# Four of sixteen gate blocks move into a Strassen pass of the values' stage, and ScalarE copies the keys' second low parts

## The chip, the cores and the metric

The kernel runs on one core of one Trainium2 chip. The metric is the device time of one execution in microseconds (us); below one microsecond, nanoseconds (ns) are used. A core has a matrix engine (TensorE, in the profile PE, its weight loads PEld), a vector engine (VectorE, DVE), a scalar engine (ScalarE, ACT), GpSimd (POOL) and a sync engine (SP) whose queue issues most DMAs. TensorE multiplies a stationary 128x128 block by a moving block of up to 128x512 and adds the result up in a PSUM bank; VectorE and ScalarE read results from there. Each engine takes its own instructions in the order of its program and waits for the others by semaphores.

## The reference

One decoder layer on x of 1024 tokens by 1024 channels, all in float32. What matters here is its beginning:

```python
h = rms_norm(x, pre_mix_g)
proj = h @ w_in            # 1024 x 8192 columns
qa, ka, va, qb, kb, vb, gates = split(proj)
...
g_a, g_b = split(sigmoid(gates))     # 2 x 1024 columns
mix = (g_a * ya + g_b * yb) @ w_mix_out
```

`qa`, `ka`, `va` (512 columns each) feed four heads of differential attention ("A"), `qb`, `kb`, `vb` (1536 each) three groups of dilated window attention ("B"). Queries and keys are rotated by tables of cosines and sines. The 2048 gate columns are used only after both attentions. A convolution-gated MLP follows.

## The kernel before, in words

**Precision.** Every operand of a large product is split into a high part, rounded to the matrix engine's fast format, and a low part, the rest. `split` (line 148) makes them: ScalarE copies to the high part (line 149), VectorE subtracts for the low part (line 146). `mm3` (lines 153 to 157) then issues three matmuls: high by high, low by high, high by low.

**Projections of queries, keys and gates.** `proj_t` takes 128 columns of `w_in` as the stationary side (a unit of 128 x 1024, loaded by `load_unit` in two halves of 256 KB, each split into slots of 128x512, of which there are 6), and streams the tokens of x, in two halves of 512, over 8 blocks of the inner dimension: 2 x 8 x 3 = 48 matmuls of 128x512. The result stands with its columns on the partitions. For a gate, `put_gate` (line 248) multiplies each half by the tokens' inverse norms, `rstd_row`, on VectorE and stores it to `gt_d` by a DMA on ScalarE's queue; there are 16 gates of 128 columns. For queries and keys, `rotated` copies the partner rows on ScalarE (line 684) and uses the tables on VectorE (lines 685 to 687). The banks of these products are the three of the pool `acc`.

**Values' stage.** All 2048 columns of the values (A's 512 and B's 1536) are computed first, by Strassen's scheme with seven products instead of eight: x is cut into four blocks (two halves of the tokens by two halves of the inner dimension) and the weight likewise. The sums of x's blocks, t2, t3 and t4, and their high and low parts are made once. The weight's sums are made on VectorE while the stage runs. There are two passes of 1024 columns. `steps_v` lists the steps: a step is one of the products p1 to p7, a pass i, and one of four blocks k of the inner dimension. In each step of these two passes x is the stationary side, in four blocks of 128 tokens, and 512 columns of the weight stream: 4 x 3 = 12 matmuls. `fetch_v` fetches the weights' blocks 8 to 10 steps ahead into 14 buffers (three tags of two in `rt`, and four tiles of two halves in `tb`), `ready_v` sums and splits them 5 steps ahead, `step_v` issues the matmuls, and at a product's last step `take_v` moves the results from PSUM to `quarter`, which `put_v` stores to `v_d` on POOL's queue. Some products go on in the bank of another without clearing it (p6 in p1's, p7 and p4 behind it, p3 in p5's), so a take has to be done before the next one starts there. While this stage runs, the norms of x, the rotation tables and a few other things are made as well, and the tables are stored. During the first steps p5 and p6 of the second pass, half of x is fetched anew and split again, since p5's operand stood in its place.

**After it.** The tables are loaded into the place where t4 stood. One gate runs (`START_GATES`), then head 0's projection `proj_a(0)`. Then come the four heads of attention A; between the pieces of each head's attention, `interleave` puts the projection of the next head (p), gates (g), and loads and splits of values (v, w, x, V) as the strings of `A_FILLS` say. Before head 3's last fills, the first projection of B (P) follows. Attention B has projections as its fill, with three gates (`B_GATES`) in its last step. Then come the mixing branches, which use the gates.

**Keys of A.** For a head's two key halves, `put_k` (line 735) writes k0 and k1, each with the same 64 rows twice, by four copies on ScalarE (lines 738, 739), and l0 and l1, the low parts, also twice, by four subtractions on VectorE (line 742).

**Order.** The functions write the instructions down with priorities (`tc.high_priority` lifts some), and the framework's scheduler then fixes each engine's order by a simulated timeline. So TensorE's order may differ from the written one, and matmuls of a fill stand where those of an attention piece would have to wait.

Of the kernel before, what the change touches and what calls it, by code (L numbers as in the profile page):

```python
# [15 lines left out]
F32 = mybir.dt.float32  # L16
# [33 lines left out]
START_GATES, A_FILLS, B_GATES = 1, ("gpgg", "gpvgg", "wgpgg", "xgPVgg"), 3  # L50
# [12 lines left out]
def plan():  # L63
# [7 lines left out]
    order += [GT + i * P for i in range(2 * KC)]  # L71
# [16 lines left out]
def trunk(ctx: ExitStack, tc: tile.TileContext, a, out):  # L88
# [344 lines left out]

    def lambda_scale():
# [10 lines left out]
    with ExitStack() as st_y:  # L445
# [6 lines left out]
        def turns(pattern, *ps):  # L452

            ks = [iter(range(4)) for _ in ps]
            return [(ps[c], 1, next(ks[c])) for c in pattern]

        steps_v += [("p1", 1, k) for k in range(4)] + turns((0, 0, 1, 0, 1, 0, 1, 1), "p5", "p6")
        steps_v += turns((0, 0, 1, 1, 1, 1, 0, 0), "p3", "p7") + [("p4", 1, k) for k in range(4)]
# [14 lines left out]

        def fetch_v(n):
# [3 lines left out]
            got_v[n] = [load_raw(a["w_v"][j * 4 + k][:, (2 * i + c) * 512 : (2 * i + c + 1) * 512], next(tags), parts=1 if n else 2)  # L478
                        for c, j in which]

        def ready_v(n, w=512):
            p, _, k = steps_v[n]
            raw = got_v.pop(n)
            src = wz[k] if p in ("p5", "p6", "p3") else raw[0]
# [9 lines left out]
            for c in range(0, 512, w):  # L494
                marks["ACT"] = split(*(t[:, c : c + w] for t in ready[n]), src[:, c : c + w])

        def take_v(p, i, m, ps):
# [3 lines left out]
            def copy(to, r):  # L501
                if i:
# [4 lines left out]
            def add(to, r):  # L507
                if i:
# [27 lines left out]

        quarter = {(0, i): new_y(f"a{i}") for i in range(2)}
        banks = {}

        def step_v(n):  # L540
            p, i, k = steps_v[n]
            x = xs_of[p]
            if p in ("p1", "p2", "p5") and k == 0:
                left = p == "p1"
                banks[left] = ([psum() for _ in range(3)] + [psum(F32, ps_o, "o")] if left else
                               [psum(F32, q, t) for q, t in ((ps_s, "s"), (pt, "pt")) for _ in range(2)])
            use = banks[p in ("p1", "p6", "p7", "p4")]
            wh, wl = ready.pop(n)
            for m in range(4):
                tk = slice(m * P, (m + 1) * P)  # L550
                mm3(use[m], x[0][:, k, tk], x[1][:, k, tk], wh, wl, k == 0 and p in ("p1", "p2", "p5"), k == 3, p in ("p6", "p7", "p4", "p3"))
            if k < 3:
                return
            with tc.high_priority(offset=80):
                for m in range(4):
# [58 lines left out]
        places_y = {("p6", 1): (1, "a0", yv), ("p5", 1): (3, "b3", yw), ("p4", 1): (2, "b2", yw)}  # L614
        quarter.update({(q, 0): new_y(f"b{q}", yw) for q in range(1, 4)})
        for n in range(8, len(steps_v)):
# [29 lines left out]
            if k == 3 and i and p in ("p1", "p7", "p4", "p3"):  # L646
                put_v({"p1": 0, "p7": 3, "p4": 2, "p3": 1}[p], 1, p == "p1")
            if (p, i) == ("p5", 1):

                again.append(load_raw(a["xT"][k][:, 512:], next(tags)))  # L650
            if (p, i) == ("p6", 1):
# [72 lines left out]
    def proj_a(h, res):  # L724
# [10 lines left out]
        def put_k(half, sl, ps):  # L735
# [4 lines left out]
            for part, kk, ll in ((u, k0, l0), (v, k1, l1)):  # L740
# [1006 lines left out]
```

## Time and profile before

| | us |
|---|---|
| median of 3 runs | 1703.26 (1700.04 to 1705.16) |
| the profiled execution | 1702.22 |
| its span, first to last instruction | 1700.3 |
| TensorE busy | 1683.2 |
| VectorE busy | 1346.2 |
| ScalarE busy | 887.9 |
| end of the values' stage | 161.9 |
| first score of attention A | 202.70 |

The profile is a hardware trace of one execution. A line of a group names the line of code, the engine, the operation, the tiles (out<-in), the shapes and how often it ran; behind the bar stand its busy time, the mean ns of one, and the engine's idle time before it with what ended that. A line of a stretch gives its bounds, its length, the busy time and count of each engine (PE, PEld, DVE, ACT, POOL), the granted clock, the share of the DMA engines, and GB/s. A line of the timeline gives start, duration, engine, line, operation and tiles, and in brackets the idle time before. A line of a fetch gives the queue, the count, the size and the median us from issue to landing. Matmuls overlap, so their durations are longer than the distance from one start to the next.

### The profile page before, as it was taken

How to read it: one execution, taken by the hardware profiler on the slowest of the kernel's cores; microseconds unless marked ns; L12 is line 12 of the kernel's file. 1: busy time of each engine (PE TensorE's matmuls, PEld its weight loads, DVE VectorE, ACT ScalarE, POOL GpSimd, SP SyncE). 2: the span in 40 equal slices, each digit the busy share in tenths (PEclk: the TensorE clock that was granted, in tenths of full speed). 3: DMA queues.
4: the chain of work that ended last, by engine and by line, in shares of the span. 5: the costliest groups of instructions: out<-in, count | busy, mean ns of one | idle time of the engine just before them, and what ended most of it. 6: DMA issues, size and time to landing. Idle time of an engine off the chain costs nothing.

```text
span 1700.3 us, 23030 instructions
## 1 busy us (share of the span) xinstructions
PE 1683.2 (99%) x8076; PEld 1408.5 (83%) x8076; DVE 1346.2 (79%) x2557; ACT 887.9 (52%) x1631; POOL 109.1 (6%) x174
## 2 busy tenths in 40 slices
PE   9999999999999999999999999999999999999997
PEld 7888888888888888888888788888888888888886
DVE  8795687877777776677756865899999989799977
ACT  7633575655544776667553433454444444355453
POOL 0031000000000000000123400300000000000000
PEclk9999999999999999999999999999999999999999
DMA  8767311213112213243675532122222222296524
GB/s 270 229 224 267 99 55 62 88 56 118 50 63 81 69 57 108 81 130 101 219 266 184 196 112 75 38 101 91 99 75 81 86 90 92 76 351 213 201 76 161
DMA packets 104451, 216.41 MB, mean 127 GB/s; under 512 B 12992, under 2 KB 22144, under 8 KB 104336
## 3 DMA queue, kind: packets, MB, share of 16 engines
q1 hardware_dynamic: 89296, 171.28, 30.3%
q0 software_dynamic: 10288, 35.28, 6.2%
q10 hardware_dynamic: 4752, 8.39, 1.3%
q8 instruction: 63, 1.03, 0.3%
q14 instruction: 52, 0.43, 0.1%
HBM read 167.05 MB, written 47.86 MB: 126 GB/s over the span
## 4 chain that ended last, share of the span: by engine, by line
PE 86%; DMA 5%; DVE 5%; issue 2%; ACT 1%; POOL 1%; SPq 0%; DVEq 0%; POOLq 0%; ACTq 0%
PE acc L155 19%; PE acc L157 19%; PE acc L156 19%; PE acc L1583 3%; PE acc L1582 3%; PE acc L1581 3%; PE o L710 2%; PE pt L697 2%; PE acc L1262 2%; PE acc L1261 2%; PE acc L1260 2%; PE o L713 1%; DVE wlo L146 1%; DMA raw<-in_w_v 1%; PE s L766 1%
## 5 line engine op out<-in xcount | busy, mean ns | idle before, releaser
L155 PE MATMUL acc<-xh,whi 128*128 128x512 f32 x768 | 304.2, 396 | 0.0
L157 PE MATMUL acc<-xl,whi 128*128 128x512 f32 x768 | 303.8, 396 | 0.0
L156 PE MATMUL acc<-xh,wlo 128*128 128x512 f32 x768 | 303.1, 395 | 0.0
L149 ACT ACTIVATE whi<-raw 128x512 fp32r<-128x512 f32 (+1 forms) x252 | 155.7, 626 | 183.7 <-PE acc L157 101.2
L146 DVE TENSOR_TENSOR wlo<-raw,whi 128x512 fp32r<-128x512 f32 (+1 forms) x252 | 182.2, 730 | 39.2 <-ACT whi L149 35.0
L157 PEld LDWEIGHTS acc<-xl,whi 128*128 128x128 f32 x768 | 144.4, 188 | 27.8
L156 PEld LDWEIGHTS acc<-xh,wlo 128*128 128x128 f32 x768 | 144.5, 188 | 27.6
L155 PEld LDWEIGHTS acc<-xh,whi 128*128 128x128 f32 x768 | 144.4, 188 | 27.5 <-DVE t L685 0.2
L155 PE MATMUL acc<-mh,whi 128*128 128x512 f32 x400 | 155.8, 390 | 0.3 <-ACT mh L149 0.3
L156 PE MATMUL acc<-mh,wlo 128*128 128x512 f32 x400 | 155.6, 389 | 0.0
L157 PE MATMUL acc<-ml,whi 128*128 128x512 f32 x400 | 155.3, 389 | 0.0
L684 ACT ACTIVATE t<-acc 64x512 f32<-64x512 f32 (+1 forms) x160 | 94.7, 592 | 58.9 <-PE acc L157 57.0
L1458 DVE TENSOR_TENSOR u<-acc,u 128x512 f32<-128x512 f32 x133 | 91.8, 695 | 23.2 <-PE acc L157 23.1
L149 ACT ACTIVATE whi<-s 128x512 fp32r<-128x512 f32 x76 | 46.9, 627 | 102.9 <-PE acc L157 88.7
L685 DVE TENSOR_TENSOR t<-acc,cos 128x512 f32<-128x512 f32 x64 | 44.2, 691 | 58.9 <-ACT t L684 56.4
L155 PEld LDWEIGHTS acc<-mh,whi 128*128 128x128 f32 x400 | 75.1, 188 | 16.2 <-ACT mh L149 0.5
L157 PEld LDWEIGHTS acc<-ml,whi 128*128 128x128 f32 x400 | 75.1, 188 | 15.6
L156 PEld LDWEIGHTS acc<-mh,wlo 128*128 128x128 f32 x400 | 75.1, 188 | 15.4
L1582 PE MATMUL acc<-whi,wlo 128*128 128x512 f32 x220 | 77.6, 390 | 0.0
L1581 PE MATMUL acc<-whi 128*128 128x512 f32 x220 | 76.3, 389 | 0.0
L1583 PE MATMUL acc<-wlo,whi 128*128 128x512 f32 x220 | 73.2, 390 | 0.0
L768 DVE CUSTOM_DVE_ANT_0 s<-s,mask_a 128x512 f32<-128x512 f32 (+3 forms) x96 | 52.0, 554 | 23.2 <-PE s L766 14.6
(389 smaller groups left out, 3953.9 us busy)
## 6 DMA issues: line engine op xcount, KB each, us to landing
raw<-in_w_in SPq DMA_DIRECT2D x96, 256.0 KB, 2.9
raw<-in_w_up SPq DMA_DIRECT2D x88, 256.0 KB, 2.7
raw<-in_w_v SPq DMA_DIRECT2D x71, 256.0 KB, 4.5
raw<-c_d SPq DMA_DIRECT2D x48, 256.0 KB, 3.8
c_d<-c SPq DMA_DIRECT2D x22, 512.0 KB, 2.8
raw<-in_w_down SPq DMA_DIRECT2D x37, 256.0 KB, 4.2
v_d<-yv POOLq DMA_DIRECT2D x32, 256.0 KB, 5.1
gt_d<-gate ACTq DMA_DIRECT2D x32, 256.0 KB, 2.2
```

The costliest lines, as they stand in the source:

```text
L146: eng.tensor_tensor(lo, src, hi.bitcast(F32), op=ALU.subtract)
L149: copy = nc.scalar.activation(hi, src, AF.Copy)
L155: nc.tensor.matmul(o, sh, mh, start=first, stop=False, skip_group_check=on)
L156: nc.tensor.matmul(o, sl, mh, start=False, stop=False, skip_group_check=on)
L157: nc.tensor.matmul(o, sh, ml, start=False, stop=last, skip_group_check=on)
L684: nc.scalar.activation(t1[dst], ps[src], AF.Copy)
L685: nc.vector.tensor_tensor(t2, ps, cos[:, sl], op=ALU.mult)
L768: nc.vector.tensor_tensor_reduce(out=s_sb[:, c0:c1], in0=ps, in1=mask, scale=1.0, scalar=-3.0e38, op0=ALU.add, op1=ALU.max, accum_out=mx[: ...
L1458: nc.vector.tensor_tensor(to, made(p), x, op=ALU.add)
L1581: nc.tensor.matmul(banks[m], gh[:, tk], wh, start=f == 0, stop=False)
L1582: nc.tensor.matmul(banks[m], gl[:, tk], wh, start=False, stop=False)
L1583: nc.tensor.matmul(banks[m], gh[:, tk], wl, start=False, stop=f == NH - 1)
```

## The change

The first 512 gate columns (gates 0 to 3) are no longer projected by `proj_t`. They are appended to the values' weight array (2560 columns instead of 2048) and computed in a third pass of the values' stage, i = 2, which is half as wide: 256 columns per block. In it the sides are exchanged. The weight's part is stationary, in two blocks of 128 columns, and 512 tokens stream, so that the result has the gates' layout: 2 x 3 = 6 matmuls of 128x512 in a step, 28 steps. It uses two banks of `acc` and two of `s`. Its results are multiplied by `rstd_row` in the new `put_g` and stored to `gt_d` on POOL's queue. The renewed half of x is fetched in the third pass instead of the second. `START_GATES` is gone, and heads 0, 2 and 3 have two gates instead of three among their fills. In `put_k` each low part is subtracted once on VectorE and its second copy is made by ScalarE from the first.

```diff
-START_GATES, A_FILLS, B_GATES = 1, ("gpgg", "gpvgg", "wgpgg", "xgPVgg"), 3
+A_FILLS, B_GATES = ("gpg", "gpvgg", "wgpg", "xgPVg"), 3
...
-    order += [GT + i * P for i in range(2 * KC)]
+    order += [GT + i * P for i in range(4, 2 * KC)]
...
-        steps_v += [("p1", 1, k) for k in range(4)] + turns((0, 0, 1, 0, 1, 0, 1, 1), "p5", "p6")
-        steps_v += turns((0, 0, 1, 1, 1, 1, 0, 0), "p3", "p7") + [("p4", 1, k) for k in range(4)]
+        for i in (1, 2):
+            steps_v += [("p1", 1, k) for k in range(4)] if i == 1 else turns(2, (0, 0, 1, 0, 1, 0, 1, 1), "p2", "p1")
+            steps_v += turns(i, (0, 0, 1, 0, 1, 0, 1, 1), "p5", "p6") + turns(i, (0, 0, 1, 1, 1, 1, 0, 0), "p3", "p7")
+            steps_v += [("p4", i, k) for k in range(4)]
...
+        def width_v(i):
+            return 512 if i < 2 else 256
+
+        def blocks_v(i):
+            return range(4 if i < 2 else 2)
...
-            got_v[n] = [load_raw(a["w_v"][j * 4 + k][:, (2 * i + c) * 512 : (2 * i + c + 1) * 512], next(tags), parts=1 if n else 2)
+            w = width_v(i)
+            got_v[n] = [load_raw(a["w_v"][j * 4 + k][:, i * 1024 + c * w : i * 1024 + (c + 1) * w], next(tags), w, 1 if n else 2)
...
-            src = wz[k] if p in ("p5", "p6", "p3") else raw[0]
+            src = wz[k][:, :width] if p in ("p5", "p6", "p3") else raw[0]
...
+        def put_g(q):
+
+            c, j = q // 2, q % 2
+            for m in blocks_v(2):
+                y, sl = quarter[q, 2][m], halves()[j]
+                tt(y, y, rstd_row[:, sl], ALU.mult)
+                nc.gpsimd.dma_start(gt_d[c * 2 + m][:, sl], y)
...
+                if i == 2:
+                    banks[left] = [psum() for _ in range(2)] if left else [psum(F32, ps_s, "s") for _ in range(2)]
...
-            for m in range(4):
+            for m in blocks_v(i):
                 tk = slice(m * P, (m + 1) * P)
-                mm3(use[m], x[0][:, k, tk], x[1][:, k, tk], wh, wl, k == 0 and p in ("p1", "p2", "p5"), k == 3, p in ("p6", "p7", "p4", "p3"))
+                ops = (x[0][:, k, tk], x[1][:, k, tk], wh, wl) if i < 2 else (wh[:, tk], wl[:, tk], x[0][:, k], x[1][:, k])
+                mm3(use[m], *ops, k == 0 and p in ("p1", "p2", "p5"), k == 3, p in ("p6", "p7", "p4", "p3"))
...
-                put_v({"p1": 0, "p7": 3, "p4": 2, "p3": 1}[p], 1, p == "p1")
-            if (p, i) == ("p5", 1):
+                q = {"p1": 0, "p7": 3, "p4": 2, "p3": 1}[p]
+                put_g(q) if i == 2 else put_v(q, 1, p == "p1")
+            if (p, i) == ("p5", 2):
...
-            for part, kk, ll in ((u, k0, l0), (v, k1, l1)):
-                for to in (u, v):
-                    nc.vector.tensor_tensor(ll[to, sl], t[part], kk[part, sl].bitcast(F32), op=ALU.subtract)
+            for part, other, kk, ll in ((u, v, k0, l0), (v, u, k1, l1)):
+                nc.vector.tensor_tensor(ll[part, sl], t[part], kk[part, sl].bitcast(F32), op=ALU.subtract)
+                nc.scalar.activation(ll[other, sl], ll[part, sl].bitcast(F32), AF.Copy)
...
-        run(gates(START_GATES)[0])
```

32 lines of the change are left out of this document (18 added, 14 removed).

## The prediction

> **What bounds the kernel now.** I read the page's busy shares and slices first, then the busy times by stretch around the place of the change, then the single matmuls there.
>
> ```profile
> span 1700.3 us, 23030 instructions
> PE 1683.2 (99%) x8076; PEld 1408.5 (83%) x8076; DVE 1346.2 (79%) x2557; ACT 887.9 (52%) x1631; POOL 109.1 (6%) x174
> PE   9999999999999999999999999999999999999997
> PEclk9999999999999999999999999999999999999999
> ```
>
> TensorE is busy for 99% of the span at the full granted clock, and no slice but the last falls below nine tenths. A busy TensorE need not be at its peak, so the spacing of the matmuls has to be seen. These are the last stretch of the values' stage and the stretch behind it, and then the first matmuls of the gate that runs there now:
>
> ```profile
> 138.00:162.00 24.00, 24.00 (x107) 19.84 (x107) 15.44 (x24) 9.70 (x16) 5.03 (x10) 1.00 0.63 207
> 162.00:202.00 40.00, 40.00 (x178) 33.13 (x177) 18.36 (x29) 20.29 (x35) 2.29 (x5) 1.00 0.40 126
> ```
> ```profile
> 161.90 0.39 PE L155 MATMUL acc<-xh,whi 128*128 128x512 f32 x1
> 162.13 0.39 PE L156 MATMUL acc<-xh,wlo 128*128 128x512 f32 x1
> 162.36 0.39 PE L157 MATMUL acc<-xl,whi 128*128 128x512 f32 x1
> 162.58 0.39 PE L155 MATMUL acc<-xh,whi 128*128 128x512 f32 x1
> ```
>
> From 161.90 to 162.58 there are three steps, 0.227 us from one start to the next; the 0.39 us of each overlaps with its neighbours. In the 40 us from 162 on, 178 such matmuls stand: 40 / 0.227 = 176, so there is no hole between them. A matmul of 128x512 that is left out here therefore takes 0.227 us out of the span, if the others can close up.
>
> The Trainium skill's Perfetto Trace Analysis, section "Identifying the Most-Contended Engine", says that busy time of matmuls is a poor measure for TensorE and that the busy share of weight loads is a good one; by it a share of 83% would leave headroom. Here the trace differs: in both stretches the weight loads are at 83% (19.84 of 24, 33.13 of 40) while the matmuls start back to back.
>
> **The change, part by part.** *Matmuls.* Removed: 4 gates x 2 halves x 8 blocks of the inner dimension x 3 (high and low parts) = 192 of 128x512. Added: 7 products x 4 blocks of the inner dimension x 2 blocks of 128 gate columns x 3 = 168, also 128x512, since the weight is now the stationary side and 512 tokens stream. The difference is -24 x 0.227 = **-5.4 us**. The Trainium skill's TensorE: Matmul & The Clock Gate, Part 1, "Wait — 56ns, not 53.3ns?", gives about 215.7 ns for a warm matmul of 512 columns, which would make it -5.2 us by estimate; the trace's spacing of 227 ns decides.
>
> *What feeds the third pass.* It lasts 168 x 0.227 = 38.1 us, in 28 steps of 6 matmuls, 1.36 us each, where a step of the second pass has 12 and 2.72 us. The nearest rows for its work on VectorE and ScalarE:
>
> ```profile
> L146 DVE TENSOR_TENSOR wlo<-raw,whi 128x256 fp32r<-128x256 f32 x2 | 0.9, 426 | 2.7 <-ACT whi L149 2.7
> L149 ACT ACTIVATE whi<-raw 128x256 fp32r<-128x256 f32 x2 | 0.8, 416 | 0.8 <-DMA raw<-in_w_v 0.8
> L329 DVE TENSOR_TENSOR wz<-raw 128x512 f32<-128x512 f32 x8 | 5.6, 694 | 1.0 <-DMA raw<-in_w_v 1.0
> L503 ACT ACTIVATE yv<-s,edge 128x512 f32<-128x512 f32 x2 | 1.2, 670 | 0.0
> L367 DVE SCALAR_TENSOR_TENSOR xl<-raw,edge,xh 128x512 fp32r<-128x512 f32 x4 | 3.0, 758 | 0.0
> L371 ACT ACTIVATE xh<-raw,edge 128x512 fp32r<-128x512 f32 x4 | 2.9, 713 | 0.4 <-DMA raw<-in_xT 0.4
> L250 DVE TENSOR_TENSOR gate<-acc,rstd_row 128x512 f32<-128x512 f32 x32 | 22.0, 689 | 11.6 <-PE acc L157 11.2
> ```
>
> VectorE gets 16 sums of weights and 28 low parts of 128x256 at 0.426 (18.7 us), 6 additions of results and 8 scalings of 128x512 at 0.694 (9.7), and the 4 low parts of x, which move here from the second pass, at 0.758 (3.0): 31.4 us of 38.1, 82%. A 128x256 sum does not stand in the trace; between nothing gained by the half width (0.694, then 36 us, 94%) and 0.426 I take 0.426, which is the same operation with a rounded output. ScalarE gets 28 x 0.416 + 8 x 0.670 + 4 x 0.713 = 19.9 us, 52%. Against this the four gates no longer need 8 splits and 8 products by rstd, 16 x 0.69 = 11 us of VectorE. So no engine is over TensorE's 38.1 us, and the cover is that the operands are made 5 steps ahead: 5 x 1.36 = 6.8 us where there were 13.6. A result must leave its PSUM bank before the product that continues or reuses that bank starts; in the order written out, two steps of another product lie between each time (p2 to p5, p1 to p6, p5 to p3, p6 to p7, p7 to p4): 2.72 us where there were 5.4. One takeover needs about two operations, 1.4 us.
>
> *Fetches.* 9 blocks of weights x 4 = 36 of 128 KB instead of 8 of 256 KB, in rows of 1 KB, through 14 buffers, and the 4 fetches of x move along. The nearest sizes, the longest fetch in this stage, and what it did:
>
> ```profile
> raw<-in_w_v SPq DMA_DIRECT2D x17, 256.0 KB, 4.4
> ```
> ```profile
> 126.28 10.10 DMA raw<-in_w_v
> ```
> ```profile
> 134.59 0.69 DVE L329 TENSOR_TENSOR wz<-raw,wz 128x512 f32<-128x512 f32 x1 [3.34 <-DMA raw<-in_w_v]
> ```
> ```profile
> 137.30 0.39 PE L156 MATMUL acc<-whi,t3l 128*128 128x512 f32 x1
> 137.75 0.50 PE L157 MATMUL acc<-wlo,t3h 128*128 128x512 f32 x1
> ```
>
> The results' stores, 8 of 256 KB, move from ScalarE's queue to POOL's:
>
> ```profile
> L251 ACTq DMA_DIRECT2D gt_d<-gate x32: 326/326/327, 168.3 to 870.0; - x32
> L535 POOL DMA_DIRECT2D v_d<-yv x32 | 21.2, 665 | 68.4 <-DVE yv L534 35.2 <-DVE yv L367 20.5 <-ACT yv L503 8.5
> ```
>
> There they cost 8 x 0.665 = 5.3 us of a queue that has nothing but the values' stores here, and ScalarE is rid of 8 x 0.33; nobody waits for them before the mixing branches: 0. At 4.4 us and some 2 us of use, 14 buffers give 14 / 6.4 = 2.2 fetches per us; 40 / 38.1 = 1.05 are needed. Even at 10.1 us each it would be 14 / 12.1 = 1.16. In the second pass the fetch of 10.1 us cost TensorE 0.45 - 0.227 = 0.22 us, once. Bounds for the third pass: none at all, or each of the five takeovers of a bank late by the 3.34 us that VectorE stood waiting, with its own 1.4 us, less the cover of 2.72: 2.0 us each, 10 us. I take **+0.8**, near the low end, some four stalls of the kind that the trace shows once: a quarter to a half of the cover is gone, but the stretch behind 138 us has the DMAs at 0.63 and VectorE at 64%.
>
> *The first gate moved away from the start of attention.* Today it stands between the values' stage and head 0's projection, while the rotation tables load:
>
> ```profile
> 161.87 0.34 SPq L359 DMA_DIRECT2D cos<-tab_d  x1
> 165.99 0.43 SPq L360 DMA_DIRECT2D sin<-tab_d  x1
> ```
> ```profile
> cos<-tab_d SPq DMA_DIRECT2D x4, 128.0 KB, 5.1
> sin<-tab_d SPq DMA_DIRECT2D x4, 128.0 KB, 4.8
> ```
> ```profile
> 202.70 0.39 PE L765 MATMUL s<-k,q 128*128 128x512 f32 x1
> ```
>
> The first table load starts as the pass's last matmul ends, and the last of eight 4.1 us later; with 4.8 us to land they are there 9 us after the pass. The first projected half will be done after 24 x 0.227 = 5.4 us (now after 72, 16.3 us). TensorE doesn't wait: there are three banks, and the fourth half, at 16.3 us, is the first that needs one back. That is 7 us of cover; beyond it each us late costs one. On SP's queue the fetches for the projection stand beside the table loads; of those a few are issued before, as slots come free in the last 6.8 us. I take 0, at most 1. Then the first score: the four halves (and the gate) end at 161.90 + 144 x 0.227 = 194.6, the score starts at 202.70, 8.1 us, which matmuls of the next gate fill. They still can: a gate is 48 x 0.227 = 10.9 us.
>
> *Fewer gates among heads 0, 2 and 3 of attention A* (two instead of three each), and the keys:
>
> ```profile
> 202.00:294.00 92.00, 92.00 (x466) 78.05 (x465) 72.19 (x183) 53.47 (x100) 0.00 (x0) 1.00 0.22 72
> 294.00:368.00 74.00, 74.00 (x395) 63.38 (x394) 56.63 (x165) 41.83 (x84) 0.00 (x0) 1.00 0.23 75
> 368.00:444.00 76.00, 76.00 (x404) 64.92 (x402) 61.27 (x172) 43.37 (x86) 0.00 (x0) 1.00 0.28 87
> 444.00:560.00 116.00, 116.00 (x603) 98.62 (x602) 84.31 (x228) 59.37 (x120) 1.14 (x4) 1.00 0.20 64
> 300.00:320.00 20.00, 20.00 (x103) 16.82 (x101) 19.57 (x53) 16.95 (x31) 0.00 (x0) 1.00 0.32 105
> 380.00:400.00 20.00, 20.00 (x109) 17.05 (x108) 19.10 (x53) 17.67 (x32) 0.00 (x0) 1.00 0.56 158
> ```
> ```profile
> L742 DVE TENSOR_TENSOR l<-t,k 64x512 fp32r<-64x512 f32 x32 | 21.9, 685 | 0.5
> L738 ACT ACTIVATE k<-t 64x512 fp32r<-64x512 f32 x16 | 10.0, 628 | 3.7 <-DVE t L687 3.5
> ```
>
> A gate takes 10.9 us of TensorE and 4 x 0.69 = 2.8 us of VectorE with it. Of the keys, 16 of the 32 low parts leave VectorE (16 x 0.685 = 11 us, 2.7 per head) and come to ScalarE (16 x 0.628 = 10 us, 2.5 per head). The tightest of the stretches, the third, becomes 76 - 10.9 = 65.1 us of TensorE with 61.27 - 5.5 = 55.8 of VectorE, 86% instead of 81%; ScalarE comes to about 44.6, 69%. TensorE stayed full where VectorE was at 19.57 and 19.10 of 20. So the cover holds on average, and I take 0; ends: 0, and the rival below. The keys' chain is as long as before: four subtractions in a row (2.7 us) become a subtraction and a copy twice, the copies behind ScalarE's own four (4 x 0.63 + 0.69 + 0.63 = 3.8 against 4 x 0.69 + the first copies, about as much): 0, from -1 to +1 in all, since gates fill it.
>
> *Sum.* The profiled execution took 1702.22 us, 1.9 over its span: 1702.22 - 5.44 + 0.8 = 1697.6. It lies 1.04 below the median of the runs shown (1703.26), so the forecast for the median is **1698.6**. About 0.3%, 5.1 us, is what a measurement of this kernel can tell from no change; the bound for faster is 1698.15, and my forecast stands 0.45 us from it.
>
> **The rivals.** *Cover too thin in attention A.* In a stretch with VectorE near 98% a gate's share of TensorE (10.9 of 76, 2.9 in 20 us) goes, and only 1.4 us of VectorE (5.5 of 76) with it: 1.4 us of stall. With one such stretch in each of three heads, 4.2 us: 1702.8, no change. For it: 19.57 and 19.10. Against it: matmuls of a later gate or projection are pulled forward there. It decides where VectorE's work exceeds TensorE's over a whole head, and the worst is 86%. Chance 0.14.
>
> *Slower: the takeovers of banks in the third pass.* VectorE and ScalarE take their work in order. If one stands on a late fetch with a result's copy queued behind it, TensorE stops at the bank. It decides when the wait is over 2.72 - 1.4 = 1.3 us. At 3.34 us and five takeovers it is 10 us: 1703.26 - 5.44 + 10 = 1707.8, slower than before. For it: the wait was there in the second pass, and the cover is halved. Against it: it fell where the rotation tables are stored, which happens once. Chance 0.10, a part of it beyond 1708.4.
>
> *TensorE has headroom*, so the 24 matmuls bring nothing: 1703.3. The spacing speaks against it. 0.02. *Other order elsewhere*: the instructions are put in order as a whole, and TensorE has holes behind attention:
>
> ```profile
> 900.00:920.00 20.00, 19.21 (x85) 15.60 (x84) 13.46 (x18) 4.46 (x8) 4.88 (x11) 1.00 0.71 246
> 940.00:960.00 20.00, 19.22 (x85) 15.58 (x83) 18.30 (x20) 9.23 (x15) 11.66 (x10) 1.00 0.46 147
> 960.00:980.00 20.00, 17.46 (x74) 13.90 (x75) 12.02 (x19) 7.95 (x15) 4.53 (x3) 1.00 0.69 233
> ```
>
> These are 4.1 us; half of them could be won or lost, which makes 1696.6 or 1700.6: 0.06, two thirds of it a gain. That the change doesn't do what it says I rule out: the count of matmuls will show it.
>
> **How the numbers follow.** Forecast 0.68. Its time lies between 1697.8 (no stall) and about 1700, with the bound for faster inside: 0.36 faster, 0.32 within. Adding the rivals (0.04 faster from the order elsewhere; 0.20 within; 0.08 slower): faster 0.40, within 0.3% 0.52, slower 0.08. The three runs lie 5.1 us apart; a third of that, 1.7, is what I allow a median of three. The range goes from 1697.8 less this to the first rival's 1702.8 plus this: 1696.1 to 1704.5.
>
> **What would show it.** TensorE's count falls by 24 to 8052 (some records can be missing). The third pass runs from about 162 to 200 us with 0.227 us between starts, VectorE at about 31 of 38; the first score stands near 230. A hole over 0.5 us in that pass at a matmul into a reused bank is the second rival; holes from 230 to 560 with VectorE at 98% the first. No holes and a span longer than 1696.5 would make the sum wrong.

## The result and the profile after

| | before | after |
|---|---|---|
| median, us | 1703.55 (4 runs) | 1715.68 (4 runs, 1713.60 to 1718.26) |
| ratio | | 1.0075 [1.0063, 1.0087] |
| profiled execution, us | 1702.22 | 1716.42 |
| its span, us | 1700.3 | 1714.6 |
| mean granted clock | 0.998 | 0.991 |

The change makes the kernel slower by 0.75%, where 0.3% faster was forecast. The page of the kernel after, first its busy times, then its slices:

```profile
PE 1688.9 (98%) x8052; PEld 1414.2 (82%) x8052; DVE 1349.1 (79%) x2583; ACT 907.9 (53%) x1675; POOL 114.4 (7%) x182
PE   9999999999998999999999999999999999999997
PEclk9999999999998899999999999999999999999999
```

TensorE has 24 matmuls fewer, as forecast, and yet more busy time. The rows of slices say why: two slices, at about 515 to 600 us, fall to 8 in the granted clock, and one of them in busy time as well. At half the clock a matmul takes longer and counts as busy.

The third pass itself runs as forecast. This is the stretch in which it stands, in the columns of the prediction's stretches, then its last matmul, the first two of head 0's projection, and the first score:

```profile
162.00:200.00 38.00, 38.00 (x170) 31.46 (x169) 24.26 (x53) 15.96 (x37) 3.81 (x7) 1.00 0.51 161
```
```profile
198.61 0.39 PE L157 MATMUL acc<-t4l,whi 128*128 128x512 f32 x1
198.84 0.39 PE L155 MATMUL acc<-xh,whi 128*128 128x512 f32 x1
199.06 0.39 PE L156 MATMUL acc<-xh,wlo 128*128 128x512 f32 x1
...
227.17 0.39 PE L791 MATMUL s<-k,q 128*128 128x512 f32 x1
```

No time is lost in the pass or at its end, and the first score comes at 227.17. The time goes later, in three places of attention A and B. Stretches of the kernel after, and then the same of the kernel before:

```profile
400.00:420.00 20.00, 18.98 (x87) 15.59 (x86) 18.39 (x48) 15.10 (x26) 0.00 (x0) 0.91 0.61 167
520.00:540.00 20.00, 15.62 (x79) 14.36 (x79) 17.10 (x55) 11.81 (x27) 1.07 (x3) 0.74 0.12 35
580.00:600.00 20.00, 17.40 (x93) 15.32 (x93) 16.21 (x37) 16.16 (x40) 0.00 (x0) 0.74 0.23 79
230.00:600.00 370.00, 361.65 (x1888) 309.77 (x1887) 275.79 (x770) 224.03 (x448) 1.93 (x4) 0.97 0.21 66
```
```profile
400.00:420.00 20.00, 20.00 (x104) 17.01 (x103) 14.60 (x40) 6.44 (x15) 0.00 (x0) 1.00 0.31 103
520.00:540.00 20.00, 20.00 (x100) 16.78 (x99) 13.99 (x31) 10.21 (x17) 1.14 (x4) 1.00 0.24 79
580.00:600.00 20.00, 20.00 (x122) 17.61 (x121) 17.46 (x47) 15.74 (x36) 0.00 (x0) 1.00 0.33 107
230.00:600.00 370.00, 369.97 (x1988) 317.30 (x1988) 281.78 (x779) 208.25 (x424) 1.14 (x4) 1.00 0.23 73
```

From 230 to 600 us TensorE idles 8.35 us (370.00 - 361.65) at a mean clock of 0.97; before, it idled 0.03 at 1.00. In the first place, the end of head 2, its matmuls were (the bracket holds the idle time, and what ended it):

```profile
404.77 0.27 PE L723 MATMUL pt<-ident,s 128*128 128x128 f32 x1
406.07 1.05 PE L865 MATMUL o<-ones,sq 128*128 128x1 f32 x8 [1.02 <-ACT sq L857]
406.98 0.49 PE L155 MATMUL acc<-xh,whi 128*128 128x512 f32 x1
...
408.56 0.63 PE L155 MATMUL acc<-xh,whi 128*128 128x512 f32 x1
408.99 0.63 PE L156 MATMUL acc<-xh,wlo 128*128 128x512 f32 x1
409.41 0.63 PE L157 MATMUL acc<-xl,whi 128*128 128x512 f32 x1
```

The norm of half a head begins with sums of squares: ScalarE squares the output (`sq`, line 857), and TensorE adds the squares up with eight matmuls of one column (line 865). Here TensorE had nothing else to do until `sq` was there. Two microseconds later the matmuls of the next projection start 0.43 us apart instead of 0.227: the clock is halved. The second place is the end of head 3, first TensorE, then VectorE:

```profile
521.84 0.28 PE L792 MATMUL s<-l,q 128*128 128x256 f32 x1
523.75 1.31 PE L865 MATMUL o<-ones,sq 128*128 128x1 f32 x8 [1.63 <-ACT sq L857]
...
531.04 0.54 PE L739 MATMUL o<-pt,vl 128*128 128x128 f32 x2
534.33 0.82 PE L873 MATMUL pt<-ident,spread 128*128 128x128 f32 x4 [2.75 <-DVE spread L868]
```
```profile
530.12 1.23 DVE L146 TENSOR_TENSOR vl<-vperm,vh 128x1024 fp32r<-128x1024 f32 x1
...
531.33 1.22 DVE L146 TENSOR_TENSOR vl<-vperm,vh 128x1024 fp32r<-128x1024 f32 x1
532.47 0.16 DVE L179 TENSOR_SCALAR rhy<-rhy 128x4 f32<-128x4 f32 x1
532.55 1.29 DVE L904 TENSOR_TENSOR ql<-t,qh 128x512 fp32r<-128x512 f32 x2
533.76 0.42 DVE L868 COPY spread<-rhy 128x512 f32<-128x512 f32 x1
```

The norm's inverse root is a string of small operations on VectorE, and its last, `spread`, stands behind low parts for attention B. No matmul of a fill stands between 516.28 and 535.44: the fills were used up. Over these 20 us VectorE wasn't full, 17.10 of 20 us, 86%; but from 527 us until the spread was made it had no gap over 0.15 us, so the longest hole is time spent behind other work in its queue. The third place is attention B's first step, where a transpose comes two microseconds late. ScalarE, which makes its operand, worked without a gap from 582.4 us until then:

```profile
584.30 0.44 PE L739 MATMUL o<-pt,vl 128*128 128x128 f32 x2
586.67 1.09 PE L723 MATMUL pt<-ident,bs 128*128 128x128 f32 x4 [1.93 <-ACT pt L149]
```

From the matmuls' starts the whole stall can be summed up: each distance from one start to the next, less the usual one of its shape (0.227 us for 512 columns, 0.119 for 256, 0.113 for 128). Between 200 and 860 us it is 2.5 us before and **22.7 us** after; 9.5 of the 22.7 are matmuls at half clock (23.9 us of the time in these stretches run at it), 13.2 are holes. Between 860 and 1070 it is 6.3 and 5.3. So -5.4 for the matmuls, +20.2 and -1.0 make +13.8 of the 14.3 us by which the spans differ. In the eight holes over 0.15 us between 230 and 600 us VectorE was busy for 7.4 of 8.2 us, 90%, against 75% over the whole of these 370 us.

### The profile page after: what moved, and what is told of

Its sections match the earlier page's. It is cut to its first block, busy times and chain, and to the rows that moved or that the text cites. A ratio compares the mean times of both kernels' runs of the same rounds, so it can differ in the third digit from the quotient of the medians.

```text
span 1714.6 us, 23153 instructions
## 1 busy us (share of the span) xinstructions
PE 1688.9 (98%) x8052; PEld 1414.2 (82%) x8052; DVE 1349.1 (79%) x2583; ACT 907.9 (53%) x1675; POOL 114.4 (7%) x182
## 4 chain that ended last, share of the span: by engine, by line
PE 92%; DVE 3%; DMA 2%; ACT 1%; issue 1%; SPq 0%; POOL 0%; DVEq 0%; ACTq 0%; POOLq 0%
PE acc L155 20%; PE acc L157 20%; PE acc L156 20%; PE acc L1608 3%; PE acc L1607 3%; PE acc L1606 3%; PE o L736 2%; PE pt L723 2%; PE acc L1287 2%; PE acc L1285 2%; PE acc L1286 2%; PE s L156 1%; PE s L157 1%; PE s L155 1%; PE o L739 1%; PE s L792 1%
## 5 line engine op out<-in xcount | busy, mean ns | idle before, releaser
L155 PE MATMUL acc<-xh,whi 128*128 128x512 f32 x712 | 283.8, 399 | 0.0
L157 PE MATMUL acc<-xl,whi 128*128 128x512 f32 x712 | 282.4, 397 | 0.0
L156 PE MATMUL acc<-xh,wlo 128*128 128x512 f32 x712 | 282.2, 396 | 0.0
L155 PEld LDWEIGHTS acc<-xh,whi 128*128 128x128 f32 x712 | 134.9, 190 | 26.0
L157 PEld LDWEIGHTS acc<-xl,whi 128*128 128x128 f32 x712 | 134.7, 189 | 26.3
L156 PEld LDWEIGHTS acc<-xh,wlo 128*128 128x128 f32 x712 | 134.9, 189 | 25.7
L736 PE MATMUL o<-pt,vh 128*128 128x256 f32 (+1 forms) x376 | 68.9, 281 | 0.3 <-ACT osb L1036 0.2
```

Of the source, the lines that this page charges most:

```text
L155: nc.tensor.matmul(o, sh, mh, start=first, stop=False, skip_group_check=on)
L156: nc.tensor.matmul(o, sl, mh, start=False, stop=False, skip_group_check=on)
L157: nc.tensor.matmul(o, sh, ml, start=False, stop=last, skip_group_check=on)
L736: nc.tensor.matmul(o[:, q0 : q1 + 1], vs[b // 4][0][:, b % 4, c], t[:, part], start=first and n == part == 0, stop=False)
```

## The experiments

My theory after the result: the gates among attention A's fills were what TensorE did while attention's steps went round between TensorE, VectorE and ScalarE, so taking three of them away saves little, and the holes and the halved clock cost the rest. The rivals: the keys' copies, the new order that the scheduler makes after any edit, a local lack of fills at the places of the holes, VectorE's load, and the norms' steps at which TensorE waits. The stall in the table is summed as above, from the one profiled execution of each kernel; "gates" are those ahead of A, in A and in B's last step, beside the 4 of the third pass.

| kernel | gates | median, us (runs) | ratio to before | stall 200-860 (half clock) | 860-1070 |
|---|---|---|---|---|---|
| before | 1+12+3 | 1702.4 to 1703.9 | | 2.5 (0) | 6.3 |
| after | 0+9+3 | 1715.68 (4) | 1.0075 [1.0063, 1.0087] | 22.7 (9.5) | 5.3 |
| keys alone | 1+12+3, no pass | 1707.33 (9) | 1.0024 [1.0015, 1.0034] | 6.7 (1.3) | 5.3 |
| keys back | 0+9+3 | 1722.33 (4) | 1.0113 [1.0098, 1.0128] | 27.4 (7.7) | 8.2 |
| fills alone | 4+9+3, no pass | 1724.53 (4) | 1.0127 [1.0112, 1.0142] | 22.6 (7.2) | 6.6 |
| fills back | 0+12+3 | 1730.23 (4) | 1.0162 [1.0145, 1.0179] | 1.9 (0) | 7.9 |
| head 0 bare | 0+9+3 | 1715.89 (1) | | 23.1 (7.0) | 5.3 |
| head 1 gives | 0+9+3 | 1718.78 (1) | | 23.5 (6.9) | 6.5 |
| late heads | 0+9+3 | 1717.2 (1) | | 21.8 (4.1) | 7.3 |
| B gives two | 0+11+1 | 1712.92 (1) | | 11.9 (4.2) | 11.7 |
| B bare | 0+12+0 | 1709.88 (4) | 1.0046 [1.0031, 1.0061] | 7.8 (2.9) | 13.1 |
| GpSimd's low parts | 0+9+3 | 1713.75 (4) | 1.0069 [1.0054, 1.0084] | 22.6 (6.9) | 3.8 |
| bare matmuls | 0+9+3 | 1727.24 (4) | 1.0145 [1.0128, 1.0162] | 14.2 (3.9) | 9.1 |
| no gates in A | 13+0+3, no pass | 1767.0 (2) | 1.0374 [1.0344, 1.0404] | 64.0 (18.9) | 8.3 |
| norms later | 0+9+3 | 1711.1 (7) | 1.0043 [1.0029, 1.0057] | 13.1 (1.4) | 5.2 |
| norms later, 11 | 0+11+1 | 1707.21 (7) | 1.0027 [1.0016, 1.0038] | 6.1 (1.4) | 12.0 |
| norms later, 10 | 0+10+2 | 1705.71 (10) | 1.0014 [1.0004, 1.0023] | 14.5 (4.0) | 2.6 |
| norms later alone | 1+12+3, no pass | 1701.73 (10) | 0.9995 [0.9986, 1.0005] | 2.2 (0) | 5.6 |

### The change taken apart

**Keys alone**: the kernel before with the new `put_k`.

```diff
-            for part, kk, ll in ((u, k0, l0), (v, k1, l1)):
-                for to in (u, v):
-                    nc.vector.tensor_tensor(ll[to, sl], t[part], kk[part, sl].bitcast(F32), op=ALU.subtract)
+            for part, other, kk, ll in ((u, v, k0, l0), (v, u, k1, l1)):
+                nc.vector.tensor_tensor(ll[part, sl], t[part], kk[part, sl].bitcast(F32), op=ALU.subtract)
+                nc.scalar.activation(ll[other, sl], ll[part, sl].bitcast(F32), AF.Copy)
```

> The kernel before with the keys' copies alone moved to ScalarE. If the stalls of the changed kernel (holes at 404, 517 to 538 and 580 to 596 us, some 20 us in all with the half clock behind them) come from gates missing among the heads (cover theory), this kernel has its 13 gates there and stays at 1703.5 within 3 us, without new holes. If they come from ScalarE's longer chain behind the keys (keys theory), it is slower by 10 to 20 us. If any change of the program reshuffles the order and brings such stalls (order theory), it is slower by an amount that has nothing to do with where the gates are.

Measured: 1707.33, +4.1 us against 1703.24 in the same batch, where my theory allowed 3 us and no new holes. Its stall grows by 4.2 us, all of it in attention B's first step, at 575 to 586 us. **Keys back**: the kernel after with the old four subtractions, the same edit the other way round.

> The changed kernel with all low parts of the keys on VectorE again. Cover theory: 1712 to 1719, with holes at the ends of heads 2 and 3 and in the first step of attention B. Keys theory: the holes go, about 1698. Order theory: holes, but in other places, and a time anywhere between 1698 and 1720.

Measured: 1722.33, 6.6 us above the kernel after, and more than the 1712 to 1719 of my theory. So the keys' copies aren't what makes the kernel after slow: in it they are a gain, where in the kernel before they are a loss. Why they are a loss there stays open. The fills back run, below, has the same copies with all twelve gates in A, and no hole in B's first step. The order that the scheduler makes of each program may be worth such a few us; that wasn't tried by itself.

**Fills alone**: the kernel before with the gates placed as the change does, four ahead of A instead of a third pass.

```diff
-START_GATES, A_FILLS, B_GATES = 1, ("gpgg", "gpvgg", "wgpgg", "xgPVgg"), 3
+START_GATES, A_FILLS, B_GATES = 4, ("gpg", "gpvgg", "wgpg", "xgPVg"), 3
```

> The kernel before with the changed kernel's fills: four gates run in a block behind the values' stage (START_GATES 4) and the heads get 2, 3, 2 and 2 gates. No third pass, no change of the keys, the same matmuls as before. Cover theory: the same holes at the ends of heads 2 and 3 and in the first step of attention B, 15 to 25 us slower than before, 1718 to 1728. If the third pass itself or the keys are the cause, it stays at 1703.5.

Measured: 1724.53, +21.3 us with the very same matmuls, and with holes in the same three places. **Fills back**: the kernel after with twelve gates in A again. Gates 4, 5 and 6 are computed twice, so that there are enough of them; that is 144 matmuls, 32.7 us, of extra work.

```diff
-A_FILLS, B_GATES = ("gpg", "gpvgg", "wgpg", "xgPVg"), 3
+A_FILLS, B_GATES = ("gpgg", "gpvgg", "wgpgg", "xgPVgg"), 3
...
-    free_gates = list(range(4, 2 * KC))
+    free_gates = [4, 5, 6] + list(range(4, 2 * KC))
```

> The changed kernel with the fills of the kernel before: three gates are computed a second time, so that the heads have 3, 3, 3 and 3 gates again (32.6 us of extra matmuls). Cover theory: the holes go; 1703.5 - 10.9 for the gate at the start + 38.1 for the third pass = 1730.7, within 4 us. If the holes have another cause they stay and it is 1715.7 + 32.6 = 1748.

Measured: 1730.23, and in attention A and B's first step the holes and the half clock are gone. The same three places of this kernel:

```profile
400.00:420.00 20.00, 20.00 (x100) 16.77 (x99) 18.49 (x52) 17.01 (x30) 0.00 (x0) 1.00 0.24 81
520.00:540.00 20.00, 20.00 (x117) 17.49 (x116) 15.12 (x50) 11.57 (x26) 0.00 (x0) 1.00 0.15 53
580.00:600.00 20.00, 20.00 (x119) 17.52 (x118) 11.11 (x33) 13.98 (x36) 0.00 (x0) 1.00 0.11 37
```

The two runs settle where the time goes. The missing gates make the stall without the rest of the change, and it goes when they are put back. And with cover in A the rest of the change brings what was forecast for it: 1703.24 - 5.4 + 32.7 = 1730.5.

### Where the gates are missed

**Head 0 bare**, **head 1 gives** and **late heads** have nine gates in A as the change has, in other heads; **B gives two** has eleven, and one in B.

```diff
-A_FILLS, B_GATES = ("gpg", "gpvgg", "wgpg", "xgPVg"), 3
+A_FILLS, B_GATES = ("p", "gpvgg", "wgpgg", "xgPVgg"), 3
...
+A_FILLS, B_GATES = ("gpg", "gpvg", "wgpg", "xgPVgg"), 3
...
+A_FILLS, B_GATES = ("gp", "gpvg", "wgpgg", "xgPVgg"), 3
...
+A_FILLS, B_GATES = ("gpg", "gpvgg", "wgpgg", "xgPVgg"), 1
```

> The changed kernel, the same twelve gates dealt out otherwise: heads 0 to 3 get 0, 3, 3 and 3 gates, the last step of B three. If a hole belongs to the head whose gate is gone (local cover), the holes near 404, 517 to 538 and 580 to 596 us go (20 us), and head 0 with its projection alone gets holes between 230 and 310 us, 5 to 15 us: 1700 to 1710. If what counts is the sum of the gates in attention A wherever they stand (total cover), the holes stay near head 3 and the first step of B: 1712 to 1720.

> The changed kernel with 2, 2, 2 and 3 gates among the heads: head 1 gives one to head 3. Local cover: the holes at the end of head 3 and in the first step of B shrink from some 18 us to under 5, the one at the end of head 2 stays (3 us) or grows, and the end of head 1 near 330 may get one of a few us: 1701 to 1708. Total cover: 1712 to 1720.

> The changed kernel with 1, 2, 3 and 3 gates among the heads, in head 0 ahead of the projection. Local cover: no holes at the ends of heads 2 and 3 and in the first step of B, a few us at the ends of heads 0 and 1: 1698 to 1706. Total cover: 1712 to 1720.

> The changed kernel with 2, 3, 3 and 3 gates among the heads and one gate in the last step of B instead of three. Either cover theory: the holes up to 600 us go, nearly (20 us less), and the last step of B, near 830 to 870 us, loses 21.8 us of cover and gets holes of 5 to 15 us: 1700 to 1711.

Measured: 1715.89, 1718.78 and 1717.2 (one run each), with a stall of 23.1, 23.5 and 21.8 us that lies at 378 to 402 us, at 391 to 409 and at 375 to 400, and each time again between 570 and 597. So the lack isn't local: nine gates in A leave 22 to 24 us of stall whichever heads they stand in. My reading, which no run tries by itself, is that the scheduler pulls later fills forward, and the shortage shows where there are none left. With eleven gates the stall is 11.9 us, about half, where I had expected it to go almost wholly (1700 to 1711, against 1712.92), and B's end lacks its own: 11.7 us between 860 and 1070. **B bare** gives all twelve to A and none to B:

```diff
-A_FILLS, B_GATES = ("gpg", "gpvgg", "wgpg", "xgPVg"), 3
+A_FILLS, B_GATES = ("gpgg", "gpvgg", "wgpgg", "xgPVgg"), 0
```

> The changed kernel with all twelve gates in attention A (3, 3, 3, 3) and none in the last step of B: the gates that the third pass saves are then the one at the start and B's three. Total cover: no stalls over 3 us up to 840 us, as in the run with three gates computed twice; the stretch from 860 to 1070 us loses its cover, where 11.7 us of stall stood with one gate left and 6 with three, so 12 to 20 now: 1703.5 - 5.4 + 6 to 14 = 1704 to 1712. If the stalls up to 600 us come with the third pass itself, they stay: over 1720.

Measured: 1709.88. A's stall is gone; most of the 7.8 us stands in B's last step, from 840 us on, and 13.1 us behind it. The gates are needed in both places.

**No gates in A**: the kernel before with the twelve gates of A ahead of it.

```diff
-START_GATES, A_FILLS, B_GATES = 1, ("gpgg", "gpvgg", "wgpgg", "xgPVgg"), 3
+START_GATES, A_FILLS, B_GATES = 13, ("p", "pv", "wp", "xPV"), 3
```

> The kernel before with the same 16 gates, the same matmuls and the same keys, but the twelve gates of attention A run in front of it, so that 13 stand between the values' stage and head 0 and none among A's fills (3 stay in B). In attention A's 302 us of before 12 x 10.9 = 131 us were gates, so 171 us of other TensorE work stay there. Theory (a chain of steps between engines sets a floor of about 290 to 300 us for attention A, and gates fill it for nothing): TensorE stands still for most of the 120 to 131 us that are left open, the half clock behind the holes comes to it, and the time is 1800 to 1840; if the shortfall only costs what three gates less did, 6.7 us each, 12 x 6.7 = 81, it is 1780 to 1790. Rival (VectorE's load sets the floor: about 234 us of VectorE in A, of which the gates' 12 x 2.8 = 33 leave with them, so 201 us): A is 201 us long instead of 171, and the time is 1733. Rival (the place of gates is of no matter, as I predicted when I took 0 for the missing gates): 1703.

Measured: 1767.0, +63.3 us, between the figures of the theories, and none of them. That is 5.3 us for each gate, where the first three (fills alone) cost 7.1 each. Attention A (first to last score) took 247 us here and 302 before. So there is no floor of 290 us, but VectorE's 201 us aren't one either. The whole of A in this kernel and one head of it, and what TensorE waited for from 333 to 610 us, the three largest (sum, times, longest):

```profile
408.00:461.00 53.00, 44.89 (x227) 37.75 (x227) 43.47 (x150) 30.57 (x69) 0.00 (x0) 0.82 0.16 50
333.00:580.00 247.00, 222.54 (x1103) 184.88 (x1101) 206.11 (x605) 157.46 (x311) 0.00 (x0) 0.90 0.14 43
```
```profile
PE pt L697 <- DVE s L784: 12.1, 8, 2.8
PE s L765 <- DVE mx L768: 4.9, 10, 1.1
PE o L839 <- ACT sq L831: 4.1, 5, 1.4
```

VectorE is at 83% (206.11 of 247), ScalarE at 64%, and TensorE stands still for 24.5 us with its clock at 0.90. No engine is full over this stretch, and in TensorE's holes over 0.15 us VectorE is busy for 20.0 of 23.8 us, 84%, no more than elsewhere in it. So the reading is that attention's own steps take turns, score, maximum, exponential, scaling, transpose, and that the gates hid it.

### VectorE's load, and work that isn't gates

**GpSimd's low parts**: in `proj_t` the low part of each unit's second half is subtracted by GpSimd.

```diff
-                split(hi[:, sl], lo[:, sl], raw)
+                split(hi[:, sl], lo[:, sl], raw, nc.gpsimd if pool_low and sl.start else None)
...
-        wh, wl = load_unit(w_in[where[col]])
+        wh, wl = load_unit(w_in[where[col]], pool_low=True)
```

> The changed kernel with the low part of every second half of the weights of queries, keys and gates subtracted on GpSimd instead of VectorE: some 26 of 52 subtractions of 0.69 us in attention A's stretch, 18 us, leave VectorE. If the uncovered stretches wait for VectorE's work above all, the stalls of 20 us shrink by a third or more: 1703 to 1710. If they wait for the chain of steps from engine to engine, whatever VectorE carries, it stays at 1712 to 1718; if GpSimd's slower subtraction holds up the weights, it is slower.

Measured: 1713.75, with the stall as it was (22.6 us). But this wasn't a test of a lighter VectorE. 44 subtractions, 44 x 0.687 = 30 us, left it, and its busy time over the whole span stayed (1349.1 after, 1352.2 here), as other operations took longer meanwhile. The rotation's sum and its product by the cosines on VectorE, in the kernel after and then in this one, and GpSimd's subtractions:

```profile
L711 DVE TENSOR_TENSOR t<-acc,cos 128x512 f32<-128x512 f32 x64 | 44.0, 690 | 63.0 <-ACT t L710 58.2 <-DMA cos<-tab_d 4.3
L713 DVE TENSOR_TENSOR t<-t,t 128x512 f32<-128x512 f32 x64 | 43.9, 687 | 0.4
```
```profile
L711 DVE TENSOR_TENSOR t<-acc,cos 128x512 f32<-128x512 f32 x64 | 44.0, 690 | 52.3 <-ACT t L710 48.0 <-PE acc L156 3.1 <-PE pt L723 0.7
L713 DVE TENSOR_TENSOR t<-t,t 128x512 f32<-128x512 f32 x64 | 61.0, 954 | 0.7
```
```profile
L146 POOL TENSOR_TENSOR wlo<-raw,whi 128x512 fp32r<-128x512 f32 x44 | 69.7, 1585 | 485.2 <-ACT whi L149 471.2 <-PE pt L1063 13.9
```

**Bare matmuls**: the kernel after with 72 matmuls of 128x512 (16.3 us) whose result nobody reads, 24 among the fills of head 2 and 48 among those of head 3.

```diff
-A_FILLS, B_GATES = ("gpg", "gpvgg", "wgpg", "xgPVg"), 3
+A_FILLS, B_GATES = ("gpg", "gpvgg", "wgpgd", "xgPVgdd"), 3
...
+    def bare():
+        ps = psum()
+        for n in range(8):
+            for _ in range(3):
+                nc.tensor.matmul(ps, xh[:, n, :P], xh[:, n, :512], start=True, stop=True)
+            if n % 2:
+                yield 0.5
...
+                "d": lambda: (bare(), 2),
```

> The changed kernel with 72 added matmuls whose result nobody reads, 24 among head 2's fills and 48 among head 3's: 16.3 us of TensorE's work without weights to split or results to move. If the half clock behind the holes is a cost of its own (9.5 of the 22.7 us of stall by the trace), the added matmuls fill the holes and keep the clock: 1705 to 1712, faster than without them. If only the holes count, filling them changes nothing: 1714 to 1718. If the holes come elsewhere than the matmuls stand, up to 1732.

Measured: 1727.24, 11.6 us more than the kernel after. The stall fell from 22.7 to 14.2 us, so of 16.3 us of work about half was covered; behind the attentions, from 860 to 1070 us, 3.8 us came to it. That is the third of the cases that I had expected, holes elsewhere than the matmuls, and it doesn't tell what the half clock costs by itself. Where the 72 stand (duration, first and last start):

```profile
L892 PE MATMUL acc<-xh x72: 387/389/452, 414.9 to 498.9; 128*128 128x512 f32 x72
```

The last one starts at 498.9, ahead of the end of head 3: they wait for nothing and are put early. Even so the holes at the end of head 3 are gone (none over 0.15 us stands between 407 and 578 us), as matmuls of projections which the 72 put off stand there now. But the hole of 1.02 us at the end of head 2 lies ahead of the first of the 72 and stays, and B's first step has holes as before, at 578 to 598 us. Where the cover stands counts, and not only its sum.

### The norms' steps

**Norms later**: the kernel after, its sums of squares one piece of attention later and the transposes of the norm two.

```diff
-        later(1, sums)
-        later(3, norm)
+        later(2, sums)
+        later(5, norm)
```

> The changed kernel with the two steps of the norm behind each half head put off: the sums of squares by one piece of attention more (2 instead of 1), the transposes by two more (5 instead of 3). TensorE waited at these steps at 404.77 and 521.84 for the square and at 531.25 for the spread. If these steps are the cause, their holes (1.0, 1.6 and 2.8 us) and the half clock behind them (3.4 + 6.8 + 3.4 us at half clock, in which some 5.5 us of work are lost) go, 10.9 us, and the time is about 1705. If the sum of other work in attention A is what is missing (the theory that the runs with the gates placed otherwise bore out), the same stall of 20 to 23 us turns up at the steps that wait next (scores, exponentials, transposes), and the time stays at 1713 to 1719.

Measured: 1711.1 over seven runs, 4.6 us below the kernel after, and between the two expectations. The stretch of the profiled run, which at 1705.05 us is the fastest of the seven, and what TensorE waited for in it, the longest first:

```profile
230.00:600.00 370.00, 364.33 (x1941) 310.11 (x1940) 280.71 (x789) 231.34 (x464) 2.30 (x4) 1.00 0.21 69
```
```profile
PE o L736 <- ACT pt L149: 1.1, 1, 1.1
PE o L736 <- DVE pt L146: 1.0, 1, 1.0
PE o L736 <- ACT osb L1036: 0.8, 1, 0.8
```

The holes stay, 11.7 us instead of 13.2, and turn up at the steps that wait next: that part is the missing cover. But in this run only 1.4 us go to half clock instead of 9.5. The runs of this one program differ, with the same instructions in the same order (us, and the mean granted clock):

```
1705.05  0.997
1707.17  0.997
1707.60  0.996
1711.10  0.994
1711.19  0.993
1712.57  0.995
1714.63  0.991
```

From 0.997 to 0.991 over some 1709 us are 10.3 us of clock, and the times differ by 9.6. So the time goes largely with the clock from run to run, though not wholly (1712.57 has 0.995). The six other runs have no trace, so their holes aren't known; and the slowest has the clock of the kernel after, so the delay doesn't do away with the half clock.

**Norms later, 11** and **norms later, 10** have eleven and ten of the twelve gates in A besides; **norms later alone** is the kernel before with the two lines above.

```diff
-A_FILLS, B_GATES = ("gpg", "gpvgg", "wgpg", "xgPVg"), 3
+A_FILLS, B_GATES = ("gpg", "gpvgg", "wgpgg", "xgPVgg"), 1
...
+A_FILLS, B_GATES = ("gpg", "gpvgg", "wgpg", "xgPVgg"), 2
```

> The changed kernel with the norms put off as in the last run, and 11 of the 12 gates in attention A, 1 in the last step of B. Without the delay this spread took 1712.9 us (one run), with 11.9 us of stall between 200 and 860 us and 11.7 behind. If the total of cover counts and the delay only spares the half clock (4.2 us lost of the 11.9 there), 1706 to 1710. If the norms' steps were the cause of A's stall, A's stall goes to 3 and the time is 1702 to 1705.

> The same with 10 gates in A and 2 in B's last step. The total of cover: between the run with 9 and 3 (1711.1) and that with 11 and 1, 1707 to 1711, no better than before. Norms as the cause: 1698 to 1703, where the sum of the prediction lies.

> The kernel before with the norms put off alone. All theories that need missing cover for the delay to matter: no change, 1701 to 1705. If the norms' steps cost TensorE something that fills hide in the profile (a floor of A that holds with the cover too), it is faster, under 1699.

Measured: 1707.21, 1705.71 and 1701.73. The delay does nothing that can be told from no change where the cover is there (0.9995 [0.9986, 1.0005]). The gates in A don't settle the stall between 200 and 860 us alone: with the delay it is 13.1 us with nine, 14.5 with ten and 6.1 with eleven. Ten gates and the delay bring the change to 1.0014 of the time before, below what was expected of the total of cover (1707 to 1711) and above what was expected of the norms as the cause (1698 to 1703). That is the best that I found; none of the versions with the third pass beats the kernel before.

## Why the prediction was wrong

**The bound** was right: TensorE back to back at 0.227 us, and 24 matmuls fewer (8052). The run with the fills back shows that they are worth their 5.4 us as long as nothing else opens up.

**The third pass** was forecast at +0.8 and cost nothing; even the hole of 0.22 us at 137.75 is gone. VectorE's work for it came to 31.2 us, as reckoned, and the sums of 128x256 that were in doubt took 0.42 us each; part of it was done ahead of the pass, so between 162 and 200 us VectorE was busy for 24.3 us and not for about 31. The rival of late takeovers didn't come: no hole stands in the pass.

**The first gate and the tables** were right at 0. The first score came at 227.17, near the 230 forecast.

**The step that failed** is the one on fewer gates among heads 0, 2 and 3: "So the cover holds on average, and I take 0". It cost 20.2 us. The sum took VectorE's busy share of a stretch (86%) for the measure of cover, as if TensorE could be short only where another engine is full. With no gates in A VectorE is at 83% and TensorE still waits: what keeps it waiting is the turn of small steps between three engines, with what stands ahead of a step in its engine's queue, and what hid that were the gates. The row that was quoted as comfort, TensorE full beside a VectorE at 19.57 of 20, showed that fills were at hand there, not that they could be spared. Of three gates, 32.7 us, which left A, 20.2 came back as stall.

**The first rival** had the place and the direction, not the price. It reckoned one stretch of each of three heads short by 1.4 us, 4.2 in all, against a measured 20.2, and made its case depend on VectorE exceeding TensorE over a whole head. Three things were missing in it. The shortage adds up over all of A, since later matmuls are pulled forward (the point that was put against the rival), so it falls on the ends of heads 2 and 3 and on B's first step, where nothing is left to pull. No engine has to be full over a whole head; waits of single steps are enough. And behind the holes the clock is halved: 9.5 of the 22.7 us. It was told as no change, so the range ended at 1704.5, 11 us short.

**The keys** were taken at 0, from -1 to +1. They are +4.1 us in the kernel before and -6.6 in the kernel after, and in fills back, with twelve gates in A, nothing is left for them to cost. So "gates fill it" wasn't enough: the 4.1 us came with all gates in place, in B's first step, and what made them is open.

**The stores on POOL's queue** and the stretch behind the attentions were right at about 0: the stall from 860 to 1070 us went from 6.3 to 5.3.

**Open** is how much of the chain is VectorE's load and how much the mere turns of the steps. The run meant to lighten VectorE didn't; the keys' copies, which take 11 us from it, make the stall 4.7 us shorter where the cover is missing (27.4 to 22.7), but they shorten the keys' steps as well. That VectorE was busy for 90% of the time of the holes in the kernel after speaks for its load, that it was busy for no more than its usual share without gates in A speaks for the turns. Which holes set off the half clock was seen, not tried by itself.

## What to carry to other kernels

Where one engine is always busy because filler work stands in the waits of a chain of steps, the filler isn't a cost that can be saved there: take it out, and the chain's waits appear, so price it by the run with and without it, not by the engines' busy shares. Work that is made cheaper should be taken from a stretch whose waits are already covered by something else, and the cover has to stand where the waits are, as well as suffice in sum. A matrix engine that falls into small holes pays twice when its clock follows.

## What the runs showed of the hardware

The clock halves after short holes. At the end of head 2 an idle time of 1.0 us at 404.8 and eight matmuls of one column were followed by 3.41 us at half clock from 408.34; behind the holes at 521.8 and 531 it was 6.83 and 3.41 us, behind B's first step 10.24. All are multiples of 3.41 us, and the matmuls of 512 columns stand 0.427 us apart in them. Their starts lie on one grid: 524.40, 534.64 and 585.84 us are 34, 37 and 52 times 3.413 us behind the first. The 3.41 us ahead of the first hold the idle time, the eight narrow matmuls, and back-to-back matmuls of 512 columns from 406.98 on. The Trainium skill's TensorE: Matmul & The Clock Gate, Part 1, "What's actually happening", gives a free-running window of 3413 ns and says that the clock falls after at least one idle window; the length of the windows and the grid agree with the trace, but no hole here lasted a whole window (the longest in A and B's first step is 2.75 us), so less than that was enough here. That the holes fall differently on this grid from run to run would fit the spread of one program's runs from 1705.05 to 1714.63 us, but only one of them has a trace here, so that isn't shown.

VectorE and GpSimd slow each other. While GpSimd did 44 subtractions at 1.585 us each, VectorE's sum of two operands in SBUF went from 0.687 to 0.954 us: the 24 that overlapped one of these took 1.402 us, the 40 others 0.685. Its product of a PSUM bank by a table stayed at 0.690 us. GpSimd's subtraction took 1.285 to 1.297 us in the three in which VectorE did nothing, and 1.72 to 1.75 in the 23 that began with 0.57 to 0.59 us of VectorE's product of two operands in SBUF still to run. That agrees with the Trainium skill's SBUF — State Buffer, "SBUF: two separate sides", by which an operation of VectorE with two inputs in SBUF and one of GpSimd that reads SBUF exclude each other. So 30 us taken from VectorE in this way freed none.
